# A gate stage's last pair: product and embedding in interleaved halves, the embedding weight's split parts kept in memory, the short tile's embedding packed

## The chip, the cores and the metric

One core of a Trainium2 chip runs the kernel. Its engines work at the same time and wait for each other by semaphores: PE (TensorE, matrix products, with PEld for its weight loads), DVE (VectorE), ACT (ScalarE), POOL (GpSimd) and SP (SyncE, which here only issues DMAs). The metric is device microseconds of one execution, as the median of several runs.

## The reference

One layer over 2048 prompt frames and 32 decode frames, D = 1024, in fp32:

```python
h = h + concat([yA, yB]) @ w_out            # yA, yB: mixers on rmsnorm(h) @ w_in
gate = sigmoid(rmsnorm(h, g_ple) @ w_ple_gate)
h = h + (p_i @ w_ple) * gate                # p_i has 256 columns
y = rmsnorm(h, g_final)
```

The mixers (a short gated convolution and a multi-scale pooling) and their states are not touched by the change. It lies in the last three lines: the embedding product `p_i @ w_ple`, the gate product, and the final norm.

## The kernel before

The rows are cut into 17 tiles: 16 of 128 prompt rows (0 to 15) and one of the 32 decode rows (16, "the short tile"). PE works in fp32r, a shorter format than fp32. So an fp32 operand is split into a high part (an ACT cast, L79) and a low remainder (a DVE subtraction, L82), and a product is made of three: high by high, high by low and low by high, all into one PSUM bank of 512 columns.

The stages follow each other in PE's queue: the input projection in three groups of column blocks ([0, 1], [2, 3], [4]) up to about 538 us, the embedding of the first three tiles, the output projection, the embedding of the rest (about 708 to 745 us), the gate stage.

**Embedding.** `embedding_weights` (L1095, called by `early_embedding` in the third group) loads the 256 rows of w_ple as two tiles of 128x1024 and splits each: `wp[k][0]` is the high part, `wp[k][1]` the low part of half k. `embedding_chunks` does the same for the later products ("wq") and once more for the last pair ("wl"). The split activations of tile i lie in memory as `pp_d[i]`, 128x512: part a, half k, row n. `embed_product` (L103) makes one half of a tile, 512 output columns, in 6 matmuls: 2 halves k times 3 products. `embed` evicts each bank by an ACT copy (L142) and stores the tile to `e_d`. For the short tile the stationary operand has 32 columns instead of 128, and its part of `pp_d` is loaded and stored as 4 pieces of 32 numbers in each of 128 rows.

**Gate stage.** First the decode tile (`plain`, `packed`: a 64-column stationary operand holds high and low side by side, L265, then 32 columns, L268). Then seven pairs of tiles (0, 2, ..., 12) in a loop, then `last_pair` with tiles 14 and 15. Each pair takes `seven` (L205): seven half-size products by a Strassen-Winograd scheme, each of 12 matmuls of 512 columns, in three banks X, Y, Z:

- X = A11·W11, copied by ACT as carry c_00 (L1501); Y = A12·W21, to which `out` adds c_00: output (row tile 0, column half 0);
- X += S2·T2, copied as c_01; Z = S1·T1, copied as c_11; Z += S4·W22, `out` with c_01: output (0, 1);
- X += S3·T3, `out` with c_11: output (1, 1); X += A22·T4, `out` with no carry: output (1, 0).

Hooks (`between`) run at numbered steps between the products. `out` of `gate_ops` adds the carry (DVE, L1509), takes the sigmoid (ACT, L1510), multiplies by the embedding row e (L1512) and adds into h (L1513). `done_g` (L1516) ends a tile: square with a sum (ACT), two small POOL operations, one DVE multiply of 128x1024 (L1520), and a store by POOL (L1521). The h rows of the tiles live in a ring, so SP's load of a later h waits for the store of an earlier tile. `prep_g` makes the next pair's operands inside the present pair: PE transposes through `turned` (L1481), and then splits and differences on DVE and ACT.

In `last_pair` (L1541) the embedding of tile 15 isn't taken from `e_d` but multiplied on the spot: 512 columns between S3's and T4's products, and 512 columns in two banks of 256 behind T4. `finish` (L1567) does the multiply and the add into h, `norm` the square (L1575), the product with g_final (L1581), the POOL sums and root (L1585 to L1591), the scaling by the root (DVE L1595, ACT L1597) and the stores (L1596, L1598).

Tile order on each engine is set by a scheduler of the framework; `tc.keep_in_program_order` pins an instruction to its place in the program.

## Time and profile before

| | us |
|---|---|
| median of 3 runs | 923.92 (922.3 to 926.05) |
| the profiled execution, its own time | 925.15 |
| its span in the trace | 923.4 |
| granted TensorE clock, mean | 0.998 |
| last e_l matmul issued, modelled end | 916.06 |

An engine's row in a timeline gives the start, the duration, the line, the operation with output and inputs, and how many instructions were drawn together; in brackets stands how long the engine had been idle before, and what released it. A list of waits says by engine and line for whom it waited: the sum, how often, the longest. Matmuls overlap in PE's pipeline: one of 512 columns shows 0.39 us, while the next starts 0.23 us later, so a group's cost is the distance to the start of the next group.

### The profile page before, as it was taken

The numbers are of one execution on the slowest core, as the hardware profiler recorded it, in microseconds if no ns is written. First come the engines' busy times: TensorE is split into PE (matmuls) and PEld (weight loads), VectorE is DVE, ScalarE is ACT, GpSimd is POOL, SyncE is SP. The second block draws the span as 40 slices with busy tenths as digits, with TensorE's granted clock in tenths as the row PEclk, the third lists the DMA queues.
The fourth block names the chain that finished last, engine by engine and source line by source line (L and its number), as shares of the span: only waits on it lengthen the run. The fifth ranks groups of instructions, "written<-read, shape, count | busy, mean of one in ns | idle before, by whom it ended". The sixth has DMA issues, their size and how long they took to land.

```text
span 923.4 us, 13197 instructions
## 1 busy us (share of the span) xinstructions
PE 908.2 (98%) x4521; PEld 823.2 (89%) x4521; DVE 723.8 (78%) x1237; ACT 483.5 (52%) x895; POOL 160.5 (17%) x303
## 2 busy tenths in 40 slices
PE   8999999999999999999999999999999999999996
PEld 6999998999999999999999987888878868888885
DVE  6996898999576989795777669665558658889885
ACT  6744565654345555443545446334336755565563
POOL 2111222121000332210000010111203201111123
PEclk9999999999999999999999999999999999999999
DMA  8357687898945799638975359866777964676653
GB/s 245 100 143 218 168 247 224 244 281 283 417 138 170 236 237 229 213 124 292 273 240 171 104 206 270 271 184 186 222 241 232 371 233 137 230 255 199 204 195 114
DMA packets 137679, 201.98 MB, mean 219 GB/s; under 512 B 13116, under 2 KB 101724, under 8 KB 136333
## 3 DMA queue, kind: packets, MB, share of 16 engines
q1 hardware_dynamic: 117581, 138.36, 48.4%
q0 software_dynamic: 17296, 57.35, 19.2%
q10 hardware_dynamic: 2736, 5.44, 1.8%
q8 instruction: 35, 0.57, 0.3%
q14 instruction: 31, 0.25, 0.1%
HBM read 135.55 MB, written 65.54 MB: 218 GB/s over the span
## 4 chain that ended last, share of the span: by engine, by line
PE 76%; DVE 6%; DMA 3%; issue 1%; ACT 1%; POOL 1%; POOLq 0%; DVEq 0%; ACTq 0%
PE x_g L162 9%; PE x_o L162 8%; PE x_zab L574 6%; PE e L106 5%; PE x_zbv L574 5%; PE z_g L162 4%; PE x_ch L574 4%; PE z_o L162 4%; PE z_zab L574 3%; PE z_zbv L574 2%; PE z_ch L574 2%; PE y_g L162 2%; PE y_o L162 2%; PE h L574 2%; PE zb L574 2%; PE c L574 2%
## 5 line engine op out<-in xcount | busy, mean ns | idle before, releaser
L79 ACT CAST y_S<-y_fS 128x512 fp32r<-128x512 f32 x32 | 19.5, 622 | 42.2 <-PE x_o L162 20.4
L162 PE MATMUL x_g<-wg_b,g_S 128*128 128x512 f32 x128 | 36.7, 392 | 0.0
L106 PE MATMUL e<-wq,pps 128*128 128x512 f32 (+1 forms) x156 | 36.2, 391 | 0.1
L162 PE MATMUL x_o<-wo_b,y_S 128*128 128x512 f32 x128 | 35.8, 391 | 0.0
L106 PEld LDWEIGHTS e<-wq,pps 128*128 128x128 f32 (+1 forms) x156 | 28.2, 182 | 7.5 <-issue 0.5
L574 PE MATMUL x_zab<-B,w_zab_S 128*128 128x416 f32 x168 | 34.2, 352 | 0.2 <-ACT V L970 0.2
L574 PE MATMUL z_zab<-B,w_zab_S 128*128 128x416 f32 x168 | 34.3, 351 | 0.0
L574 PE MATMUL x_zbv<-B,w_zbv_S 128*128 128x416 f32 x168 | 34.2, 352 | 0.0
L574 PE MATMUL z_ch<-B,w_ch_S 128*128 128x416 f32 x168 | 34.1, 351 | 0.0
L574 PE MATMUL z_zbv<-B,w_zbv_S 128*128 128x416 f32 x168 | 34.0, 351 | 0.0
L574 PE MATMUL x_ch<-B,w_ch_S 128*128 128x416 f32 x168 | 34.0, 351 | 0.0
L574 PEld LDWEIGHTS x_zab<-B,w_zab_S 128*128 128x128 f32 x168 | 31.3, 188 | 0.9 <-ACT V L970 0.5
L574 PEld LDWEIGHTS x_ch<-B,w_ch_S 128*128 128x128 f32 x168 | 31.4, 188 | 0.3
L574 PEld LDWEIGHTS z_zbv<-B,w_zbv_S 128*128 128x128 f32 x168 | 31.4, 188 | 0.3
L574 PEld LDWEIGHTS z_ch<-B,w_ch_S 128*128 128x128 f32 x168 | 31.3, 188 | 0.3
L574 PEld LDWEIGHTS z_zab<-B,w_zab_S 128*128 128x128 f32 x168 | 31.3, 188 | 0.3
L574 PEld LDWEIGHTS x_zbv<-B,w_zbv_S 128*128 128x128 f32 x168 | 31.3, 188 | 0.4
L79 ACT CAST y<-y 128x512 fp32r<-128x512 f32 x24 | 14.8, 618 | 29.6 <-PE z_o L162 12.8
L71 POOL TENSOR_SCALAR ms_f<-ssq_f 128x1 f32<-128x1 f32 (+1 forms) x15 | 7.6, 509 | 129.4 <-ACT junk L92 129.4
L1315 DVE TENSOR_TENSOR c_o<-x_o,x 128x512 f32<-128x512 f32 x14 | 9.7, 690 | 25.0 <-PE x_o L162 25.0
L162 PEld LDWEIGHTS x_o<-wo_b,y_S 128*128 128x128 f32 x128 | 23.9, 188 | 5.6 <-ACT y_S L79 0.4
L162 PEld LDWEIGHTS x_g<-wg_b,g_S 128*128 128x128 f32 x128 | 23.7, 188 | 4.7
(587 smaller groups left out, 2688.8 us busy)
## 6 DMA issues: line engine op xcount, KB each, us to landing
y<-y_d SPq DMA_DIRECT2D x16, 512.0 KB, 6.0
x<-in_x_prompt_dram SPq DMA_DIRECT2D x16, 512.0 KB, 5.9
h_d<-x SPq DMA_DIRECT2D x16, 512.0 KB, 4.6
h<-h_d SPq DMA_DIRECT2D x16, 512.0 KB, 3.5
xt<-in_x_prompt_dram SPq DMA_DIRECT2D x15, 512.0 KB, 7.1
e<-e_d SPq DMA_DIRECT2D x15, 512.0 KB, 4.8
out_dram<-h POOLq DMA_DIRECT2D x14, 512.0 KB, 3.1
p_dT<-T POOLq DMA_DIRECT2D x12, 512.0 KB, 6.4
```

Source lines behind the costliest of these rows:

```text
L71: nc.gpsimd.tensor_scalar(ms[:n], ssq[:n], scalar1=1.0 / D, scalar2=EPS, op0=ALU.mult, op1=ALU.add)
L79: ins = nc.scalar.copy(hi, src)
L106: nc.tensor.matmul(ps[:n], pps[:, a, k, :n], wp[k][b][:, cs], start=k + q == 0, stop=k == 1 and q == 2)
L162: nc.tensor.matmul(ps[:n], lhs[:, k, a, :n], w[b][:, k], start=start and k + q == 0, stop=k == KH - 1 and q == 2, skip_group_check=True)
L574: nc.tensor.matmul(ps[:, :NB], lhs[:, k, x], b[:, k, y], start=start and k + q == 0, stop=stop and k == KH - 1 and q == 2, skip_group_chec ...
L1315: add = lambda o, a, b: nc.vector.tensor_tensor(o, a, b, op=ALU.add)
```

## The change

- The short tile: its split activations are laid out so that for each half k the 32 high and the 32 low columns lie side by side; load and store move 128 runs of 512 bytes. `short_embed_product` multiplies the 64 columns by the high part of w_ple and the 32 high ones by its low part: 4 matmuls for each 512 output columns. The eviction is an ACT copy of rows 0 to 31 and a DVE add of rows 32 to 63.
- The split parts of w_ple made in the third group are stored to `wl_d` by four stores of 512 KB on POOL's queue. `last_pair` loads them (two on SP at each of the steps 1 and 2) in place of raw rows, casts and subtractions.
- `last_pair`: T4's product and the following embedding product are made in two parts of 256 columns, in turn (`end`), the sigmoid with them. c_11's copy is kept in program order; row 0's first square and weighing come at step 4, the embedding of the upper half at step 5, and `done_g` of tile 13 moves from behind its pair to step 3 of the last pair.

```diff
--- before.py
+++ after.py
@@ -44,6 +44,7 @@
     h_d = tc.dram_tile([T, D], F32, name="h_d")
     e_d = tc.dram_tile([T, D], F32, name="e_d")
     g_d = tc.dram_tile([D, D], F32, name="g_d")
+    wl_d = [[tc.dram_tile([P, D], F32, name=f"wl_d{k}{h}") for h in range(2)] for k in range(2)]
     x4_d = tc.dram_tile([4, P, D], F32, name="x4_d")
     pp_d = tc.dram_tile([NT, P, 2 * PLE], F32, name="pp_d")
@@ -100,10 +101,10 @@
     def rows_of(pr, sa, r, n):
         return pr[r:r + n] if r < SEQ else sa
-    def embed_product(ps, pps, wp, cs, n=P):
+    def embed_product(ps, pps, wp, cs):
         for k in range(2):
             for q, (a, b) in enumerate(((0, 0), (0, 1), (1, 0))):
-                nc.tensor.matmul(ps[:n], pps[:, a, k, :n], wp[k][b][:, cs], start=k + q == 0, stop=k == 1 and q == 2)
+                nc.tensor.matmul(ps, pps[:, a, k], wp[k][b][:, cs], start=k + q == 0, stop=k == 1 and q == 2)
     def load_ple(t, k):
@@ -112,10 +113,17 @@
             nc.sync.dma_start(t[q * 32:q * 32 + 32], w_ple[r:r + 32])
     def load_pps(t, i, queue):
-        n = tiles[i][1]
-        queue.dma_start(t.rearrange("p a k n -> p (a k) n")[:, :, :n].bitcast(F32),
-                        pp_d[i].rearrange("p (a n) -> p a n", a=4)[:, :, :n])
+        n = 4 * tiles[i][1]
+        queue.dma_start(t.rearrange("p a k n -> p (a k n)")[:, :n].bitcast(F32), pp_d[i, :, :n])
         return t
+    def short_embed_product(ps, pps, wp, cs, n):
+        a = pps.rearrange("p a k n -> p (a k n)")[:, :4 * n].rearrange("p (k m) -> p k m", k=2)
+        for k in range(2):
+            for b, m in ((0, 2 * n), (1, n)):
+                nc.tensor.matmul(ps[:m], a[:, k, :m], wp[k][b][:, cs], start=k + b == 0, stop=k + b == 2,
+                                 skip_group_check=True)
     def embed(todo, wp, ring, queue=nc.sync, loads=nc.sync):
@@ -138,7 +146,12 @@
             for nh in range(2):
                 cs = slice(nh * NH, nh * NH + NH)
                 ps = bank(f"e_{i}_{nh}")
-                embed_product(ps, pps, wp, cs, n)
+                if n < P:
+                    short_embed_product(ps, pps, wp, cs, n)
+                    nc.scalar.copy(o[:n, cs], ps[:n])
+                    nc.vector.tensor_tensor(o[:n, cs], ps[n:2 * n], o[:n, cs], op=ALU.add)
+                    continue
+                embed_product(ps, pps, wp, cs)
                 (nc.vector.tensor_copy if last and nh else nc.scalar.copy)(o[:n, cs], ps[:n])
             (nc.gpsimd if last else queue).dma_start(e_d[r:r + n], o[:n])
@@ -202,7 +215,8 @@
         return A, more
-    def seven(name, A, W, carry, out, between={}, late=False, in_parts=False, first_tile=False):
+    def seven(name, A, W, carry, out, between={}, late=False, in_parts=False, first_tile=False, end=None):
@@ -253,6 +267,9 @@
         if not first_tile:
             right()
         step(6)
+        if end is not None:
+            end(X)
+            return
         product(X, A["22"], W["T4"], P, False)
         out(X, None, (1, 0))
@@ -1099,6 +1116,9 @@
                 load_ple(raw, k)
                 t = [wtile(f"{name}{k}_{h}").rearrange("p k h n -> p (k h n)") for h in range(2)]
                 split(t[0], t[1], raw)
+                for h in range(2):
+                    nc.gpsimd.dma_start(wl_d[k][h], t[h].bitcast(F32))
                 wp.append(t)
             return wp
@@ -1223,16 +1243,16 @@
                     for c in range(2 if w == D else 1):
                         i = a + b + c
                         n = tiles[i][1]
-                        o = s[:, c * 2 * PLE:(c + 1) * 2 * PLE].rearrange("p (a k n) -> p a k n", a=2, k=2)[:, :, :, :n]
+                        flat = s[:, c * 2 * PLE:c * 2 * PLE + 4 * n]
                         if n == P:
+                            o = flat.rearrange("p (a k n) -> p a k n", a=2, k=2)
                             src = v[:, (b + c) * PLE:(b + c + 1) * PLE].rearrange("p (g k r) -> p k g r", g=4, k=2)
                             hi, lo = (o[:, h].rearrange("p k (g r) -> p k g r", g=4) for h in range(2))
                         else:
                             src = v.rearrange("p (k r) -> p k r", k=2)
-                            hi, lo = o[:, 0], o[:, 1]
+                            hi, lo = (flat.rearrange("p (k a n) -> p a k n", a=2, k=2)[:, h] for h in range(2))
                         split(hi, lo, src)
-                        nc.gpsimd.dma_start(pp_d[i].rearrange("p (a n) -> p a n", a=4)[:, :, :n],
-                                            o.rearrange("p a k n -> p (a k) n").bitcast(F32))
+                        nc.gpsimd.dma_start(pp_d[i, :, :4 * n], flat.bitcast(F32))
                     yield
         def at_pace(steps, num, den):
@@ -1493,12 +1513,14 @@
             u = t.rearrange("p (g k t) -> p k g t", g=4, k=KC)
             return u[:, :KH], u[:, KH:]
+        carried = []
         def gate_ops(h, e, n, name, i):
             scale = lambda at: rs_h[:n, i + at[0]:i + at[0] + 1]
             def carry(ps, at):
                 t = st.tile([P, NH], F32, tag="t", name=f"c_{name}_{at[0]}{at[1]}")
-                nc.scalar.copy(t[:n], ps[:n])
+                carried.append(nc.scalar.copy(t[:n], ps[:n]))
                 return t
             def out(ps, c, at):
@@ -1514,9 +1536,9 @@
             return carry, out
-        def done_g(i, h):
+        def done_g(i, h, later=False):
             r, n = tiles[i]
-            rf = sumsq(h, n, f"f{i}")
+            rf = sumsq(h, n, f"f{i}", later=later)
             nc.vector.scalar_tensor_tensor(h[:n], h[:n], rf[:n], g_bc[:n], op0=ALU.mult, op1=ALU.mult)
             nc.gpsimd.dma_start(rows_of(y_p, y_s, r, n), h[:n])
@@ -1538,91 +1560,130 @@
             return carry, out
-        def last_pair(i, A):
+        def last_pair(i, A, before):
             pps = load_pps(ss.tile([P, 2, 2, P], F32R, tag="s", name="pps_l"), i + 1, nc.sync)
             e = load_rows(ya, "e", i, e_d)
...
+            wp = []
+            def chunk(k):
+                t = [cmb.tile([P, KH, 2, P], F32R, tag="c", name=f"wl_{k}_{h}").rearrange("p a b c -> p (a b c)")
+                     for h in range(2)]
+                for h in range(2):
+                    nc.sync.dma_start(t[h].bitcast(F32), wl_d[k][h])
+                wp.append(t)
             h = [load_rows(xh, "h", i + b, h_d) for b in range(2)]
             tt = nc.vector.tensor_tensor
             carry, _ = gate_ops(h, [e], P, f"g{i}", i)
             hg = [ring4(ya, f"hg_{b}") for b in range(2)]
             sums = [[], []]
...
+            fixed = lambda ins: tc.keep_in_program_order(ins)
+            def gated(b, cols, t, ee):
+                tt(t, ee, t, op=ALU.mult)
+                fixed(tt(h[b][:, cols], h[b][:, cols], t, op=ALU.add))
+            def square(b, cols):
+                ssq = sm.tile([P, 1], F32, tag="ssq", name=f"ssq_l{b}_{cols.start}")
+                fixed(nc.scalar.activation(junk[:, cols], h[b][:, cols], AF.Square, scale=D ** -0.5, accum_out=ssq))
+                sums[b].append(ssq)
+                if len(sums[b]) == 1:
                     nc.gpsimd.tensor_scalar(ssq, ssq, scalar1=EPS, scalar2=None, op0=ALU.add)
...
+                else:
+                    nc.gpsimd.tensor_tensor(ssq, ssq, sums[b][-2], op=ALU.add)
+            def weigh(b, cols, eng=nc.vector):
+                fixed(eng.tensor_tensor(hg[b][:, cols], h[b][:, cols], g_bc[:, cols], op=ALU.mult))
+            def root(b):
                 rf = sm.tile([P, 1], F32, tag="rstd", name=f"rstd_l{b}")
...
+                nc.gpsimd.tensor_tensor(rf, sums[b][-1], nhalf, op=ALU.pow)
+                return rf
+            def normed(b, rf):
                 r = tiles[i + b][0]
                 o, y = hg[b], y_p[r:r + P]
                 cut = 5 * P
...
+                fixed(nc.vector.tensor_scalar(o[:, :cut], o[:, :cut], scalar1=rf, scalar2=None, op0=ALU.mult))
                 nc.sync.dma_start(y[:, :cut], o[:, :cut])
...
+                fixed(nc.scalar.activation(o[:, cut:], o[:, cut:], AF.Copy, scale=rf))
                 (nc.scalar if b else nc.gpsimd).dma_start(y[:, cut:], o[:, cut:])
+            cols_of = lambda half: slice(half * NH, half * NH + NH)
+            at_last = {}
+            def sigmoid(o, src, b):
+                return nc.scalar.activation(o, src, AF.Sigmoid, scale=rs_h[:, i + b:i + b + 1])
             def out(ps, c, at):
                 b, half = at
...
+                tt(c, ps, c, op=ALU.add)
+                sigmoid(c, c, b)
+                cs = cols_of(half)
+                if b:
+                    at_last["gate"] = c
+                    return
+                gated(0, cs, c, e[:, cs])
+                if half:
+                    of_first(cs, nc.vector)
+                    at_last["root"] = root(0)
+            def of_first(cs, eng):
+                square(0, cs)
+                weigh(0, cs, eng)
+            def held(ps, at):
+                c = carry(ps, at)
+                if at == (1, 1):
+                    fixed(carried[-1])
+                return c
+            def rest():
+                of_first(cols_of(0), nc.gpsimd)
+            def second(cols):
+                ps = bank(f"e_l{cols.start}")[:, :cols.stop - cols.start]
+                embed_product(ps, pps, wp, cols)
+                return ps
+            def upper_half():
+                gated(1, cols_of(1), at_last["gate"], second(cols_of(1)))
+            def end(X):
+                t = st.tile([P, NH], F32, tag="t", name="g_l")
+                m = NH // 2
+                cs = [slice(o, o + m) for o in (0, m)]
+                for c, part in enumerate(cs):
+                    for k in range(KH):
+                        for a, b in FINE:
+                            nc.tensor.matmul(X[:, part], A["22"][:, k, a], W["T4"][b][:, k, part], start=False,
+                                             stop=k == KH - 1 and (a, b) == FINE[-1], skip_group_check=True)
+                    fixed(sigmoid(t[:, part], X[:, part], 1))
+                    ee = second(part)
+                    if c == 0:
+                        normed(0, at_last["root"])
+                        square(1, cols_of(1))
+                    gated(1, part, t[:, part], ee)
+                    if c == 0:
+                        weigh(1, cols_of(1))
+                for part in cs:
+                    square(1, part)
+                weigh(1, cols_of(0))
+                normed(1, root(1))
+            seven(f"g{i}", A, W, held, out, {1: lambda: chunk(0), 2: lambda: chunk(1), 3: before, 4: rest, 5: upper_half}, first_tile=True, end=end)
         def prep_g(i):
@@ -1677,9 +1738,10 @@
             h = [load_rows(xh, "h", i + b, h_d) for b in range(2)]
             e = [load_rows(ya, "e", i + b, e_d) for b in range(2)]
             seven(f"g{i}", A, W, *gate_ops(h, e, P, f"g{i}", i), prep_g(i + 2))
-            for b in range(2):
-                done_g(i + b, h[b])
-        last_pair(NT - 3, S[NT - 3])
+            done_g(i, h[0])
+            if i + 2 < NT - 3:
+                done_g(i + 1, h[1])
+        last_pair(NT - 3, S[NT - 3], lambda: done_g(NT - 4, h[1], True))
```

More of the change, by code (lines that the diff above doesn't have):

```diff
@@ L1553, in last_pair @@
             sums = [[], []]
-            gate = {}
-            def finish(b, half, parts):
-                t = gate[b, half]
-                where = []
-                for cs, ee in parts:
-                    fs = slice(half * NH + cs.start, half * NH + cs.stop)
-                    where.append(fs)
-                    for o, x, op in (t[:, cs], ee, ALU.mult), (h[b][:, fs], h[b][:, fs], ALU.add):
-                        ins = tt(o, x, t[:, cs], op=op)
-                        if len(parts) > 1:
-                            tc.keep_in_program_order(ins)
-                return lambda: norm(b, half, where)
@@ L1572, in norm @@
-            def norm(b, half, where):
-                for fs in where:
-                    ssq = sm.tile([P, 1], F32, tag="ssq", name=f"ssq_l{b}_{fs.start}")
-                    ins = nc.scalar.activation(junk[:, fs], h[b][:, fs], AF.Square, scale=D ** -0.5, accum_out=ssq)
-                    if b:
-                        tc.keep_in_program_order(ins)
-                    sums[b].append(ssq)
-                second = half != b
-                for fs in (where if b == 0 else [*where, slice(half * NH + NH, half * NH + 2 * NH)] if second else []):
-                    ins = (nc.vector if second else nc.gpsimd).tensor_tensor(hg[b][:, fs], h[b][:, fs], g_bc[:, fs], op=ALU.mult)
-                    if b:
-                        tc.keep_in_program_order(ins)
-                if not second:
-                    nc.gpsimd.tensor_scalar(ssq, ssq, scalar1=EPS, scalar2=None, op0=ALU.add)
-                    return
-                if len(where) > 1:
-                    nc.gpsimd.tensor_tensor(sums[b][0], sums[b][0], sums[b][1], op=ALU.add)
-                nc.gpsimd.tensor_tensor(ssq, ssq, sums[b][0], op=ALU.add)
+            fixed = lambda ins: tc.keep_in_program_order(ins)
@@ L1600, in out @@
+            at_last = {}
+            def sigmoid(o, src, b):
+                return nc.scalar.activation(o, src, AF.Sigmoid, scale=rs_h[:, i + b:i + b + 1])
             def out(ps, c, at):
                 b, half = at
-                if c is None:
-                    c, src = st.tile([P, NH], F32, tag="t", name="g_l"), ps
-                else:
-                    tt(c, ps, c, op=ALU.add)
-                    src = c
-                nc.scalar.activation(c, src, AF.Sigmoid, scale=rs_h[:, i + b:i + b + 1])
@@ L1608, in out @@
-                gate[at] = c
-                if b == 0:
-                    finish(b, half, [(slice(0, NH), e[:, half * NH:half * NH + NH])])()
-            def second(half, m):
-                parts = []
-                for o in range(0, NH, m):
-                    ps = bank(f"e_l{half}_{o}")
-                    embed_product(ps[:, :m], pps, wp, slice(half * NH + o, half * NH + o + m))
-                    parts.append((slice(o, o + m), ps[:, :m]))
-                return finish(1, half, parts)
```

8 lines of the change are left out of this document (removed).

## The prediction

> **What bounds the kernel now.** I read the page's shares first, then the waits of PE (TensorE) behind 690 us, where all that changes in PE's queue lies, then the timelines of the last 20 us.
>
> ```profile
> span 923.4 us, 13197 instructions
> PE 908.2 (98%) x4521; PEld 823.2 (89%) x4521; DVE 723.8 (78%) x1237; ACT 483.5 (52%) x895; POOL 160.5 (17%) x303
> ```
>
> ```profile
> PE z_g L162 <- ACT c_g L1501: 0.4, 1, 0.4
> ```
>
> PE is busy for 98%, and from 690 us on it waits once, 0.4 us. So time goes only with PE instructions, with that wait, or in the tail behind the last matmul; work that leaves another engine counts if it reaches one of these. The end:
>
> ```profile
> 901.54 2.88 PE L162 MATMUL z_g<-wg_a,g_S 128*128 128x512 f32 x12
> 904.26 1.07 PE L162 MATMUL x_g<-wg_b,g_S 128*128 128x512 f32 x4
> 905.71 3.03 PE L162 MATMUL z_g<-wg_d,g_S 128*128 128x512 f32 x12 [0.38 <-ACT c_g L1501]
> 908.58 1.98 PE L162 MATMUL x_g<-wg_b,g_S 128*128 128x512 f32 x8
> 910.39 1.52 PE L106 MATMUL e_l<-wl,pps_l 128*128 128x512 f32 x6
> 911.75 2.88 PE L162 MATMUL x_g<-wg_T,g 128*128 128x512 f32 x12
> 914.47 1.59 PE L106 MATMUL e_l<-wl,pps_l 128*128 128x256 f32 x12
> ...
> 904.46 0.63 ACT L1575 ACTIVATE junk<-h 128x512 bf16<-128x512 f32 x1 [1.18 <-DVE h L1567]
> 905.09 0.56 ACT L1501 COPY c_g<-z_g 128x512 f32<-128x512 f32 x1
> 911.59 0.73 ACT L1607 ACTIVATE c_g<-c_g,rs_h 128x512 f32<-128x512 f32 x1 [1.36 <-DVE c_g L1605]
> 912.24 0.63 ACT L1575 ACTIVATE junk<-h 128x512 bf16<-128x512 f32 x1
> 916.37 0.42 ACT L1575 ACTIVATE junk<-h 128x256 bf16<-128x256 f32 x1 [0.40 <-DVE h L1567]
> ...
> 903.60 0.69 DVE L1567 TENSOR_TENSOR h<-h,c_g 128x512 f32<-128x512 f32 x1
> 915.46 0.42 DVE L1567 TENSOR_TENSOR g_l<-e_l,g_l 128x256 f32<-128x256 f32 x1 [0.32 <-ACT g_l L1607]
> 915.91 0.42 DVE L1567 TENSOR_TENSOR h<-h,g_l 128x256 f32<-128x256 f32 x1
> 916.26 0.41 DVE L1567 TENSOR_TENSOR g_l<-e_l,g_l 128x256 f32<-128x256 f32 x1
> 916.71 0.42 DVE L1567 TENSOR_TENSOR h<-h,g_l 128x256 f32<-128x256 f32 x1
> 917.16 0.42 ACT L1575 ACTIVATE junk<-h 128x256 bf16<-128x256 f32 x1 [0.28 <-DVE h L1567]
> 919.16 0.55 DVE L1595 TENSOR_SCALAR hg<-hg,rstd_l 128x640 f32<-128x640 f32 x1 [0.73 <-POOL rstd_l L1591]
> ```
>
> The wait: the S4 product of the last pair needs bank Z, whose copy c_11 (905.09, ACT) stands behind a square (904.46) that waited for DVE's add of 903.60. The z matmuls were fed to 904.42 (901.54 + 2.88), so the copy could have run earlier. The tail: PE ends at 916.06 (914.47 + 1.59), but DVE had both 256-column parts in front of it and finished at 917.13; the last square, the sums on POOL and the scaling follow in a row.
>
> **The short tile.** Its embedding loses 4 matmuls of 12.
>
> ```profile
> L106 PE MATMUL e<-wq,pps x156: 387/389/496, 708.7 to 745.1; 128*128 128x512 f32 x144, 128*32 128x512 f32 x12
> 739.67 5.81 PE L106 MATMUL e<-wq,pps 128*128 128x512 f32 x24
> 745.32 1.08 PE L265 MATMUL x_gl<-wg_c,gl_a 128*64 128x512 f32 x4
> 746.24 1.09 PE L268 MATMUL x_gl<-wg_c,gl_a 128*32 128x512 f32 x4
> ```
>
> A matmul with 32 columns in the stationary operand moves 512 columns as a full one does, 0.235 us from start to start (745.32 − 739.67 over 24); the 64-column form that replaces it takes 0.23 (746.24 − 745.32 over 4). The last ones run at 0.227 (2.72 over 12, 911.75 to 914.47). Four fewer: **−0.91 us** (−0.94 at the slower pace). The eviction gains a DVE add of 32x512 for each half; no PE instruction waits for this tile's embedding before the end of the decode tile, and DVE is 78% busy: 0, and at most two adds of 0.69 if both ends met a full queue. Loads and stores of 128 rows by 512 B instead of 512 pieces by 128 B lie off the path: 0.
>
> **The wait.** c_11 is now kept ahead of the row-0 square, so it needs only the end of S1's product: −0.38, and the copy (0.56) is done 0.3 us before PE asks for it at 905.33 (904.26 + 1.07), all earlier by 0.91. **−0.38 us**; 0 if the square still comes first.
>
> **T4 in two parts.** 12 matmuls of 512 columns become 24 of 256. The e_l row of 12 gives (1.59 − 0.28) / 11 = 0.119 each: 24 × 0.119 = 2.86 against 2.72, **+0.14 us**. Bounds: 0 if they ran at exactly half (0.1135), +2.7 if a short one cost what a long one does, which that row speaks against.
> By the Trainium skill ("TensorE: Matmul & The Clock Gate", LDWEIGHTS (loading the stationary operand)), a weight load lasts its columns over 1.2 in ns, 107 for 128 columns. If the 12 extra loads were exposed the sum would be 1.28 us worse; the row's 0.119 a pair leaves no room for that.
>
> Both parts lie in one bank, and the changed order of PE has a wait of the second part for ACT's sigmoid of the first (as in the wait above, where a matmul waits for ACT's copy of its bank). Part one is modelled to end 1.63 after its start (12 × 0.119 + 0.16 of drain + 0.04 as from 914.63 to the sigmoid). A 256-column sigmoid is about 0.52 (0.73 less the 0.21 by which a square shrinks from 0.63 to 0.42). So it ends at +2.15, and PE, after the six embedding matmuls of part one (0.71), asks at +2.14; with 0.06 to wake up (905.09 + 0.56 to 905.71) I take **+0.06**, from 0 to +0.9 (a sigmoid that queues behind the square, rival two).
> The Trainium skill ("PSUM — Partial Sum Buffer", PSUM bank collisions raise a hardware error) says two engines may not touch one bank at once, other columns included; by that rule the wait can't be dropped, only covered, and the sum stays as it is.
>
> **The tail.** The part-one gate (multiply, add, weigh) now runs while PE does part two, so behind the last matmul stand one multiply and one add instead of a queue of four. PE end by the sum: 916.06 − 0.91 − 0.38 + 0.14 + 0.06 = 914.97; multiply at +0.09, add, square at 915.97 instead of 917.16, the rest as before: 1.19 earlier, so **−0.1** beyond PE. What could spoil it: DVE's row-0 scaling now stands ahead of part one's multiply; with the row-0 chain 1.2 earlier it runs at about 912.75 and the 512-wide weighing ends near 914.7, 0.35 before it is needed.
>
> **The embedding weight kept.** Last pair: two ACT casts and two DVE subtractions (1.06 and 1.22 us each) go, at 904.20 one right behind the add that held the wait above. Four 512 KB loads replace eight smaller. The last of the four lands in the slot of S2, free at 900.6 (901.54 − 0.91); even at 6.0 us (below) it lands at 906.7, and its matmuls start at 909.1. Each, and the h load queued behind it on SP, has over 2 us of slack: 0. In the third group:
>
> ```profile
> 532.30 1.22 DVE L82 TENSOR_TENSOR wp<-raw_wp,wp 128x1024 fp32r<-128x1024 f32 x1
> 534.71 0.50 POOL L1084 DMA_DIRECT2D out_dram<-so  x1 [25.87 <-ACT so L1082]
> 541.04 2.21 SPq L317 DMA_DIRECT2D wo_q<-in_w_out_dram  x4
> 559.44 1.42 PE L157 MATMUL y_o<-wo_c,y 128*128 128x512 f32 x5 [0.53 <-ACT wo_c L1388]
> h_d<-x SPq DMA_DIRECT2D x16, 512.0 KB, 4.6
> ```
>
> POOL stands idle there, so four stores issue as the parts are ready, the last at 533.5, ahead of the `so` stores, whose wait (ACT) ends about then. At 4.6 us, as other 512 KB stores, all are down by 538.2, before the next loads at 541.04: 0. If they drag those loads, PE's wait at 559.44 grows, at most by one store, +4.6.
>
> **Moved around in the loop.** In the changed order, for the first two changes of pair, the transposes of the next pair come later in PE's queue, and DVE's add into the odd row h precedes the subtraction that makes the next pair's A11 residue.
>
> ```profile
> 786.77 2.08 SPq L322 DMA_DIRECT2D h<-h_d  x2
> 789.68 0.69 DVE L1512 TENSOR_TENSOR e<-e,c_g 128x512 f32<-128x512 f32 x1 [0.79 <-ACT c_g L1510]
> 790.29 0.68 DVE L82 TENSOR_TENSOR g<-pth,g 128x512 fp32r<-128x512 f32 x1
> 795.09 0.68 DVE L1513 TENSOR_TENSOR h<-h,e 128x512 f32<-128x512 f32 x1
> 797.03 0.57 ACT L1501 COPY c_g<-x_g 128x512 f32<-128x512 f32 x1
> 798.96 0.39 PE L162 MATMUL x_g<-wg_a,g_S 128*128 128x512 f32 x1
> h<-h_d SPq DMA_DIRECT2D x16, 512.0 KB, 3.5
> e<-e_d SPq DMA_DIRECT2D x15, 512.0 KB, 4.8
> y<-y_d SPq DMA_DIRECT2D x16, 512.0 KB, 6.0
> ```
>
> Before, that add stood at 795.09, 5 us behind the load; now it is due at 789.4 (789.68 − 0.91 + 0.6), and the load, issued at 785.86, lands at 789.36 with 3.5 us. What hangs on it is S4's cast, then the copy of 797.03 (until 797.60), needed by PE at 798.96: 1.36 of slack, less 0.6 for the added step, 0.75. **0 us**, and each microsecond of load beyond 4.3 costs one at each of the two places.
>
> **The sum.** −0.91 − 0.38 + 0.14 + 0.06 − 0.1 = −1.2. The profiled execution took 925.15 (923.4 of span and 1.75 around it), so 923.95 by its own time; it lay 1.23 above the median of the three runs, 923.92 (922.3 to 926.05), so **922.7** as a median. That is 0.13%, inside the 0.5% (4.6 us) that a measurement can tell from no change.
>
> **Rivals.**
> *One, the loop waits for the odd row (the other side).* If the two loads take 6.0 like the y loads, each place costs 6.0 − 4.3 = 1.7, together 3.4: 926.1, slower than before. It decides from 4.9 us on (2 × 0.6 eats the gain). For it: e loads of the same size in the same burst take 4.8. Against: the h loads' own median is 3.5.
> *Two, the wait moves instead of going.* The sigmoid of part one queues behind row 0's square, or the copy behind its old square. If that square stays near 912.24 while PE runs ahead, or the c_11 wait stays, 0.4 to 0.9 is given back: about 923.4. For it: the margin at +2.14 is nil. Against: what feeds the square (z and x products) moves up with PE.
> *Three, the weight's stores cost (the kept copy doesn't save what it should).* One store on the path at 559.44: up to +4.6, 927.3; half of it, 925.0. Against: DMA has 2.8 us free before 541.04.
> *Four, more comes off than I count,* as loop waits too small for the list vanish: no row gives it over 1 us; only a disturbed comparison would bring 4.6.
>
> **How the numbers follow.** Forecast 0.57, rival one 0.17, two 0.14, three 0.08, four 0.04. The forecast's own range is 921.8 to 923.6 (its bounds and a third of the spread of the runs). Low 920.9 takes in a run at the lower end of that spread; high 926.0 reaches to rival one at 6.0 and past the middle of three. Slower by over 0.5% (928.5) needs both places beyond 7 us or three with one: 0.08. Faster by 0.5% (919.3), rival four: 0.04. Within: 0.88.
>
> **What would show it.** Eight matmuls instead of 12 with the 32- and 64-column forms, none of them idle; no wait of z_g for c_g in the last pair; T4 as 24 matmuls in 2.9 us with a wait of at most 0.1 for g_l between its halves; the last square 0.9 to 1.0 behind PE's end instead of 1.1; no wait of x_g for a cast or a copy between 745 and 830 us. Any PE wait near 778 or 798, or before 565, proves me wrong by its length.

## The result, and the profile after

| | before | changed |
|---|---|---|
| median | 923.35 us (16 runs, 922.01 to 926.05) | 921.51 us (16 runs, 920.11 to 924.25) |
| ratio to before, 95% interval | | 0.9979, 0.997 to 0.9989 |
| the profiled execution, its own time | 925.15 | 921.02 |
| its span | 923.4 | 919.2 |

The changed kernel is faster by 0.2%, 1.8 us (1.0 to 2.8 by the interval); forecast were 1.2. The two profiled executions differ by 4.1. Of that, 2.78 lie ahead of the short tile's first matmul, a place that shifts by 1.6 between two traces of the changed kernel itself (below). The page of the changed kernel, its PE timeline at the short tile and at the end, and behind the last dots the short tile of before:

```profile
span 919.2 us, 13202 instructions
PE 905.7 (99%) x4529; PEld 822.7 (90%) x4529; DVE 722.4 (79%) x1236; ACT 481.2 (52%) x894; POOL 159.8 (17%) x307
...
739.76 2.01 PE L125 MATMUL e<-wq,pps 128*64 128x512 f32 x8
741.61 1.07 PE L282 MATMUL x_gl<-wg_c,gl_a 128*64 128x512 f32 x4
...
897.64 2.88 PE L175 MATMUL z_g<-wg_a,g_S 128*128 128x512 f32 x12
900.36 1.07 PE L175 MATMUL x_g<-wg_b,g_S 128*128 128x512 f32 x4
901.27 2.98 PE L175 MATMUL z_g<-wg_d,g_S 128*128 128x512 f32 x12
904.09 1.98 PE L175 MATMUL x_g<-wg_b,g_S 128*128 128x512 f32 x8
905.90 1.53 PE L107 MATMUL e_l<-wl,pps_l 128*128 128x512 f32 x6
907.27 1.59 PE L1671 MATMUL x_g<-wg_T,g 128*128 128x256 f32 x12
908.70 0.88 PE L107 MATMUL e_l<-wl,pps_l 128*128 128x256 f32 x6
909.43 1.69 PE L1671 MATMUL x_g<-wg_T,g 128*128 128x256 f32 x12
910.96 0.88 PE L107 MATMUL e_l<-wl,pps_l 128*128 128x256 f32 x6
...
742.54 2.94 PE L106 MATMUL e<-wq,pps 128*32 128x512 f32 x12
```

From the short tile on no instruction of PE carries a wait in brackets any more, and the list of PE's waits behind 690 us is empty. The parts, each the distance between two starts or ends that stand in these rows, in those of the tail below and in those of before. The span is given to 0.1 us, so what ends with it is good to 0.05:

| part | before | changed | difference |
|---|---|---|---|
| start to the short tile's first matmul | 742.54 | 739.76 | -2.78 |
| short tile | 2.78 | 1.85 | -0.93 |
| decode tile and seven pairs, to the last S1 product | 156.22 | 156.03 | -0.19 |
| S1's start to S4's | 4.17 | 3.63 | -0.54 |
| S4's start to T4's | 6.04 | 6.00 | -0.04 |
| T4 and its embedding, to PE's modelled end | 4.31 | 4.57 | +0.26 |
| PE's end to the last add | 1.07 | 0.99 | -0.08 |
| last add to the last store's issue | 2.67 | 2.20 | -0.47 |
| that issue to the end of the span | 3.60 | 4.17 | +0.57 |

From the short tile on the sum is -1.42, from 180.86 to 179.44. This span, "short tile to end", is used below to compare traces, since what lies ahead of it scatters by more than the change is worth.

The tail of the changed kernel (DVE, ACT, POOL, and the issue of the last store), and in the second block the rows of before that answer the last two of them:

```profile
911.95 0.42 DVE L1589 TENSOR_TENSOR g_l<-e_l,g_l 128x256 f32<-128x256 f32 x1 [0.37 <-PE e_l L107]
912.40 0.43 DVE L1590 TENSOR_TENSOR h<-h,g_l 128x256 f32<-128x256 f32 x1
912.87 0.42 ACT L1594 ACTIVATE junk<-h 128x256 bf16<-128x256 f32 x1 [0.83 <-DVE h L1590]
913.52 0.19 POOL L1599 TENSOR_TENSOR ssq_l<-ssq_l,ssq_l 128x1 f32<-128x1 f32 x1 [1.15 <-ACT junk L1594]
...
915.03 0.38 ACTq L1616 DMA_DIRECT2D out_dram<-hg  x1
```

```profile
917.81 0.66 POOL L1589 TENSOR_TENSOR ssq_l<-ssq_l,ssq_l 128x1 f32<-128x1 f32 x1 [0.60 <-ACT junk L1575]
...
919.80 0.38 ACTq L1598 DMA_DIRECT2D out_dram<-hg  x1
```

One multiply and one add stand behind the last matmul, as forecast. The 0.47 between add and store came from elsewhere: the same POOL add of 128x1 takes 0.19 instead of 0.66. Before, DVE was in three 256-column products at that moment; now it has one product left, which ends as POOL begins. That this is the reason was not tried.

The loop, at the second change of pair (DVE, ACT, PE):

```profile
786.99 0.69 DVE L1535 TENSOR_TENSOR h<-h,e 128x512 f32<-128x512 f32 x1 [0.29 <-DMA h<-h_d]
...
794.19 0.57 ACT L1523 COPY c_g<-x_g 128x512 f32<-128x512 f32 x1
...
795.18 0.39 PE L175 MATMUL x_g<-wg_a,g_S 128*128 128x512 f32 x1
```

Rival one's mechanism is there: DVE waits 0.29 for the odd row. What hangs on it, the copy, ends at 794.76 and PE asks at 795.18. Of the forecast slack of 0.75 there remain 0.42, and PE loses nothing.

### The profile page after: what moved, and what is told of

It is laid out like the page before. It is cut to its first block, busy times and chain, and to the rows that moved or that the text cites. A ratio compares the mean times of both kernels' runs of the same rounds, so it can differ in the third digit from the quotient of the medians.

```text
span 919.2 us, 13202 instructions
## 1 busy us (share of the span) xinstructions
PE 905.7 (99%) x4529; PEld 822.7 (90%) x4529; DVE 722.4 (79%) x1236; ACT 481.2 (52%) x894; POOL 159.8 (17%) x307
## 4 chain that ended last, share of the span: by engine, by line
PE 91%; DVE 3%; DMA 2%; ACT 2%; issue 1%; POOL 0%; SPq 0%; POOLq 0%; DVEq 0%; ACTq 0%
PE x_g L175 9%; PE x_o L175 9%; PE x_zab L591 7%; PE x_zbv L591 6%; PE x_ch L591 5%; PE z_g L175 5%; PE e L107 4%; PE z_o L175 4%; PE z_zab L591 3%; PE h L591 3%; PE z_zbv L591 3%; PE z_ch L591 3%; PE b L591 3%; PE za L591 3%; PE zb L591 2%; PE c L591 2%
## 5 line engine op out<-in xcount | busy, mean ns | idle before, releaser
L107 PE MATMUL e<-wq,pps 128*128 128x512 f32 x144 | 33.1, 390 | 0.0
L107 PEld LDWEIGHTS e<-wq,pps 128*128 128x128 f32 x144 | 27.0, 188 | 5.6
L1542 DVE SCALAR_TENSOR_TENSOR h<-h,rstd_f,g_bc 128x1024 f32<-128x1024 f32 (+1 forms) x15 | 19.3, 1284 | 14.0 <-POOL rstd_f L76 14.0
```

The source lines that it names most:

```text
L107: nc.tensor.matmul(ps, pps[:, a, k], wp[k][b][:, cs], start=k + q == 0, stop=k == 1 and q == 2)
L1542: nc.vector.scalar_tensor_tensor(h[:n], h[:n], rf[:n], g_bc[:n], op0=ALU.mult, op1=ALU.mult)
```

## The experiments

Each kernel stands beside runs of the kernel before on its own chip. All are edits of the changed kernel, but for the first and the ninth, which are edits of the kernel before. "S1 to S4" is 3.63 where PE doesn't wait for c_11.

| kernel | median us | ratio to before, interval | short tile to end | S1 to S4 | issue to end |
|---|---|---|---|---|---|
| packed tile alone | 925.43 | 1.0024, 1.0012 to 1.0037 | 183.45 | 5.86 | 3.58 |
| last pair alone | 923.72 | 1.0005, 0.9996 to 1.0014 | 180.63 | 3.63 | 4.20 |
| weight from raw | 923.05 | 0.9994, 0.9985 to 1.0003 | 179.63 | 3.87 | 3.55 |
| square first | 925.26 | 1.0017, 1.0008 to 1.0026 | 181.68 | 5.78 | 4.15 |
| changed, again | 922.61 | 0.9989, 0.998 to 0.9997 | 179.43 | 3.62 | 4.19 |
| stores on SP | 921.46 | 0.9978, 0.9969 to 0.9987 | 178.91 | 3.63 | 3.58 |
| T4 whole | 922.67 | 0.999, 0.9973 to 1.0006 | 179.90 | 3.63 | 4.15 |
| T4's parts adjacent | 923.15 | 0.9998, 0.9989 to 1.0007 | 180.24 | 3.62 | 4.12 |
| packed, norm moved | 925.85 | 1.0013, 1.0002 to 1.0023 | 182.01 | 3.84 | 3.60 |
| norm not moved | 921.41 | 0.9965, 0.9952 to 0.9978 | 179.46 | 3.62 | 4.11 |
| parts pinned | 923.69 | 0.9994, 0.9984 to 1.0003 | 180.89 | 3.63 | 4.18 |
| 384 and 128 columns | 921.82 | 0.997, 0.9958 to 0.9982 | 179.24 | 3.62 | 3.61 |

**The packed short tile alone.**

```diff
-                embed_product(ps, pps, wp, cs, n)
+                if n < P:
+                    short_embed_product(ps, pps, wp, cs, n)
...
```

> The kernel before with the packed short tile alone. Theory A (the gain is in PE's queue at the places named: short tile 0.95, last pair's wait 0.54 with its restart, loop 0.19, less 0.26 for T4 in parts; what else lay between the two profiled executions, 2.75 us ahead of the short tile, is chance): the 8 matmuls of the short tile take about 1.85 us instead of 2.8, the wait of z_g for c_g stays with 0.3 to 0.5, the loop from the decode tile to the last pair's S1 product takes the 156.0 us of the changed kernel, since its order comes with the packing; the time is 1.0 to 1.2 below before. Theory B (the time ahead of the short tile belongs to the change, to the stores of the weight or the packed loads): with the packing alone the first matmul of the short tile would start 1 us or more earlier than in the kernel before only if the packing is what moves it.

The short tile took its 1.85, as theory A has it, and the loop 156.11 (theory A: 156.0), but the kernel is slower than before, by 2.1 us. Neither theory had that. DVE, ACT and PE in the last pair, then two DVE rows of before, and the windows of PE's granted clock (after the sums of DVE, ACT and POOL comes PEclk):

```profile
901.60 1.29 DVE L1532 SCALAR_TENSOR_TENSOR h<-h,rstd_f,g_bc 128x1024 f32<-128x1024 f32 x1 [0.73 <-POOL rstd_f L75]
903.60 1.28 DVE L1532 SCALAR_TENSOR_TENSOR h<-h,rstd_f,g_bc 128x1024 f32<-128x1024 f32 x1 [0.72 <-POOL rstd_f L75]
904.80 0.68 DVE L1617 TENSOR_TENSOR c_g<-y_g,c_g 128x512 f32<-128x512 f32 x1
...
905.52 0.72 ACT L1619 ACTIVATE c_g<-c_g,rs_h 128x512 f32<-128x512 f32 x1 [3.37 <-DVE c_g L1617]
906.15 0.56 ACT L1513 COPY c_g<-z_g 128x512 f32<-128x512 f32 x1
...
903.63 1.07 PE L174 MATMUL x_g<-wg_b,g_S 128*128 128x512 f32 x4
906.77 4.55 PE L174 MATMUL z_g<-wg_d,g_S 128*128 128x512 f32 x12 [2.07 <-ACT c_g L1513]
911.12 2.10 PE L174 MATMUL x_g<-wg_b,g_S 128*128 128x512 f32 x8
```

```profile
900.32 0.68 DVE L1605 TENSOR_TENSOR c_g<-y_g,c_g 128x512 f32<-128x512 f32 x1
...
902.40 1.28 DVE L1520 SCALAR_TENSOR_TENSOR h<-h,rstd_f,g_bc 128x1024 f32<-128x1024 f32 x1
```

```profile
906.00:908.00 2.00, 1.23 (x5) 1.06 (x6) 1.69 (x3) 1.80 (x4) 0.16 (x1) 0.98 0.82 307
908.00:910.00 2.00, 2.00 (x6) 1.50 (x6) 0.93 (x1) 0.59 (x2) 2.00 (x1) 0.50 0.55 217
910.00:912.00 2.00, 2.00 (x8) 1.58 (x7) 0.65 (x1) 0.00 (x0) 0.30 (x2) 0.67 0.00 0
```

Read from the last row upward through the engines: PE waits 2.07 for the copy c_11; the copy stands on ACT behind the sigmoid of c_00; the sigmoid waits for c_00's add; the add stands on DVE behind both multiplies with the norms of tiles 12 and 13, where before it stood ahead of the second. The packing had touched none of these. But with the packed form, 4 matmuls fewer and two adds more, the scheduler ordered the gate stage anew, and in the last pair this order came out worse. Behind the wait the 12 S4 matmuls last 4.55 instead of 2.98: the granted clock falls to 0.50. The trace is that of the slowest of seven executions; from the short tile on it is 2.6 longer than before, half a microsecond more than the medians show.

**The last pair and the kept weight alone.** The packing's hunks taken out of the changed kernel.

> The changed kernel with the short tile as before (6 matmuls for each half, 32 columns), so the kept weight and the new last pair alone. Theory A: the short tile takes 2.8 us again, the loop the 156.2 us of before, no wait of z_g in the last pair, T4 and its embedding 4.57 us; 0.3 to 0.5 below before in all. Theory B: the stores in the third group move what follows: the embedding of the first tiles, the output projection and the rest up to the short tile would be some 2 us shorter here than in the kernel before, and the time 1.5 or more below.

Theory A's parts came as listed (short tile 2.78, loop 156.25, no wait, T4 and embedding 4.59). From the short tile to the end it gains 0.23; the median shows no change. The expected 0.3 to 0.5 came to less: the end of the program, from the last store's issue, is 0.6 longer (4.20), and POOL's shorter sum gives back only 0.47 of it. So the packing alone costs 2, the last pair alone gives nothing measurable, and both together save 1.8 (1.0 when measured again).

**The weight from its raw rows.**

```diff
-            wp = []
-            def chunk(k):
...
+            wp = embedding_chunks("wl")
```

> The changed kernel without the kept weight: no stores in the third group, and the last pair loads the raw rows and splits them (two casts of 1.06 on ACT, two subtractions of 1.22 on DVE). PE's order is the same. Theory A: the kept weight alone is worth nothing on PE's path as long as c_11's copy is ahead of the square: no wait of z_g for c_g over 0.1, time within 0.5 of the changed kernel. Rival: the casts and the subtractions are what made the copy late; then PE waits 0.3 or more for c_g again and the time is 0.5 to 1 above the changed kernel.

No wait for c_11 is listed, but DVE is late for another bank: T4 waits until c_11's add has read X.

```profile
910.20 1.69 PE L1659 MATMUL x_g<-wg_T,g 128*128 128x256 f32 x12 [0.26 <-DVE c_g L1614]
```

In the last pair the raw rows cost 0.24 up to S4 and some 0.5 around T4; at the end of the program they save 0.6. The trace is 0.2 longer than the changed kernel's. The ratio is 0.5 or 1.4 us above the changed kernel's two, with intervals that overlap, so neither side of the expectation is shown by the time; in the trace the kept weight has a gain and a price of nearly the same size.

**The square first.**

```diff
-                    fixed(carried[-1])
...
-                if half:
-                    of_first(cs, nc.vector)
+                of_first(cs, nc.vector if half else nc.gpsimd)
+                if half:
```

> The changed kernel with row 0's first square back where its add is, and c_11's copy not held, so that the copy stands behind the square on ACT. Theory A: the square can't start before the add of 900.75 (as in the changed kernel's trace), the copy follows about 901.5 and ends about 902.05; PE asks at 901.5 (it does one more S3 matmul first), so it waits 0.5 to 0.6, loses 0.7 with the restart, and the time is 0.7 above the changed kernel. Rival: the add is early enough without the splitting of the weight, and no wait over 0.1 shows.

```profile
902.30 0.63 ACT L1594 ACTIVATE junk<-h 128x512 bf16<-128x512 f32 x1 [2.46 <-DVE h L1590]
903.10 1.06 ACT L93 ACTIVATE junk<-h 128x1024 bf16<-128x1024 f32 x1
904.16 0.57 ACT L1523 COPY c_g<-z_g 128x512 f32<-128x512 f32 x1
...
904.78 3.03 PE L175 MATMUL z_g<-wg_d,g_S 128*128 128x512 f32 x12 [1.77 <-ACT c_g L1523]
```

The wait returns, but of 1.77 instead of 0.5: not one square stands ahead of the copy but two, since that of tile 13, moved to step 3, is pinned behind row 0's. In the order of the changed kernel the place of the copy is worth 2.2 us, four times what the wait of before showed.

**The changed kernel again.**

> The changed kernel as it is, beside the next three on one chip. Its time 921.5 again (1.8 below before); in the trace 179.4 us from the short tile's first matmul to the end of the span, no wait of z_g for c_g, an instruction fetch of 0.01 MB behind the last store and 4.2 us from the last store's issue to the end. Theory A (what lies ahead of the short tile is chance): the start of the short tile's first matmul scatters by 1 us or more against the 739.8 us of the first trace. Theory B (the change brings it forward): it is 739.8 again within 0.3.

Short tile to end is 179.43 against 179.44, part by part the same within 0.04. The short tile begins at 741.37 instead of 739.76, a scatter of 1.6, as theory A has it, and the time is 1.0 below before instead of 1.8. So the 1.4 behind the short tile's start repeats, and the medians scatter around it, presumably by what lies ahead.

**The stores on SP's queue.**

```diff
-                    nc.gpsimd.dma_start(wl_d[k][h], t[h].bitcast(F32))
+                    nc.sync.dma_start(wl_d[k][h], t[h].bitcast(F32))
```

> The changed kernel with the four stores of the weight on SP's queue, so that POOL's program is as long as before. All three kernels with the stores on POOL end 4.15 to 4.20 us after the last store's issue, with an instruction fetch in between; the three without end 3.55 to 3.60 after it, without a fetch. Theory: POOL's longer program makes the fetch and it costs 0.6 at the end; then here 3.6 and no fetch, and the time is 0.6 below the changed kernel. Rival: the end is longer for another reason (SP's or PE's program, the loads back): 4.2 again.

The last store's issue to the end is 3.58 again, and the kernel, at 0.9978 of before, ran 1.15 us below the changed one on the same chip; the intervals overlap, the traces differ by 0.52 from the short tile on. SP's waits at the end, of the changed kernel and of this one:

```profile
SPq L1770 <- DMA out_dram<-hg: 2.2, 2, 1.8
SPq L1770 <- PEq L1770: 1.0, 2, 0.8
```

```profile
SPq L1770 <- DMA out_dram<-hg: 1.9, 2, 1.6
SPq L1770 <- PEq L1770: 0.7, 2, 0.5
```

Two halves of 0.3: SP waits longer for the last stores, and then longer for PE's queue at the very end. A window of the DMA queues over the last microseconds shows an instruction fetch in all eight traces with the stores on POOL, and in none of the six without (the row is the changed kernel's):

```profile
q14 instruction: 1, 0.01, 0.3%
```

It lands behind the end of the span, so it is a sign of POOL's longer program, and not shown to be the wait itself.

**T4 whole.**

```diff
-                for c, part in enumerate(cs):
-                    for k in range(KH):
...
+                product(X, A["22"], W["T4"], P, False)
+                fixed(sigmoid(t, X, 1))
+                for c, part in enumerate(cs):
+                    ee = second(part)
```

> The changed kernel with T4's product whole (12 matmuls of 512 columns), one sigmoid of 512, the embedding of 256 and 256 columns behind it as before. Theory A (the interleaving trades PE time for the tail): T4 with its embedding takes 4.31 instead of 4.58 us, but the last add ends 1.4 to 1.6 behind PE's end instead of 1.0, as DVE gets both parts late; the time is 0.1 to 0.4 above the changed kernel. Rival: the interleaving gives nothing, the time is 0.2 to 0.3 below it, by PE's shorter queue.

```profile
907.56 2.89 PE L175 MATMUL x_g<-wg_T,g 128*128 128x512 f32 x12
910.29 1.59 PE L107 MATMUL e_l<-wl,pps_l 128*128 128x256 f32 x12
...
913.12 0.43 DVE L1590 TENSOR_TENSOR h<-h,g_l 128x256 f32<-128x256 f32 x1
```

T4 and its embedding take 4.32, the last add ends 1.67 behind PE: 0.46 longer from the short tile on. Theory A by the trace; the medians (922.67 and 922.61) don't resolve it. By the trace the interleaving is worth about half a microsecond.

**T4's parts adjacent, then pinned.**

```diff
+                for part in cs:
...
+                            fixed(nc.tensor.matmul(X[:, part], A["22"][:, k, a], W["T4"][b][:, k, part], start=False,
...
+                for c, part in enumerate(cs):
+                    ee = second(part)
```

> The changed kernel with the two parts of T4 one right behind the other, and both parts of the embedding after them: nothing covers the sigmoid that lies between the parts in the bank. Theory A (a matmul into the bank waits until ACT has read it): x_g waits 0.6 to 0.75 for g_l between the parts, and the time is 0.6 to 0.9 above the changed kernel. Rival: the wait costs nothing, as the parts lie in different columns: no wait, and the same time.

This one (without the pins) didn't try what it should: the scheduler put five of the six embedding matmuls between the parts. It shows only that the late embedding costs 0.68 behind PE's end. With the pins:

> As the run with both parts of T4 one behind the other, but with PE's order of these matmuls pinned, since there the scheduler had put five of the embedding's six matmuls of part one between the parts, and so covered the sigmoid again. Theory A: PE waits 0.6 to 0.75 for g_l between the parts; PE's end comes 0.7 later than with the parts interleaved. Rival: no wait.

```profile
909.46 1.60 PE L1673 MATMUL x_g<-wg_T,g 128*128 128x256 f32 x12
911.62 1.69 PE L1673 MATMUL x_g<-wg_T,g 128*128 128x256 f32 x12 [0.56 <-ACT g_l L1624]
```

PE waits for the sigmoid of the other columns, 0.56 listed and 0.73 in all (911.62 against 909.46 + 1.43); T4 and its embedding take 5.29, 0.72 more than interleaved. Theory A: the six embedding matmuls between the parts cover a wait for the shared bank, which is there although the columns differ. No run leaves that wait out.

**The packed tile with only the norm moved.** In the kernel before with the packing, the end of tile 13 goes to step 3; nothing else of the new last pair.

> The packed short tile alone (as in the first of these runs, which was 2.1 slower than before) and, of the new last pair, one thing: the end of tile 13 (its square, its multiply with the norm, its store) moved from behind its pair to step 3 of the last pair. Theory: in the first run ACT's copy c_11 stood behind the sigmoid of c_00, whose add stood on DVE behind both 128x1024 multiplies with the norms of tiles 12 and 13; moved, it stands behind one. Then the add comes about 2 us earlier, PE waits 0.2 to 0.5 for c_11 instead of 2.07, the granted clock stays at 1.00 behind the wait instead of falling to 0.50 for 4 us, and the time is 3 to 4 below that run: 921.9 to 922.5. Rival: the wait comes from the splitting of the embedding weight on DVE and ACT, which stays: the wait keeps 1.5 or more.

The wait for c_11 is gone (3.84 from S1 to S4, clock 1.00), so the first chain is right: its one link undone undoes it. But the time is still above before, by 1.8 in the medians and 1.2 by the ratio, and not at the expected 921.9 to 922.5. DVE's queue is late for the next one in line, T4 (PE, then DVE):

```profile
911.02 3.02 PE L174 MATMUL x_g<-wg_T,g 128*128 128x512 f32 x12 [1.10 <-DVE c_g L1617]
...
906.51 1.23 DVE L82 TENSOR_TENSOR wl<-wlr,wl 128x1024 fp32r<-128x1024 f32 x1 [1.87 <-ACT wl L79]
908.48 1.28 DVE L1532 SCALAR_TENSOR_TENSOR h<-h,rstd_f,g_bc 128x1024 f32<-128x1024 f32 x1 [0.75 <-POOL rstd_f L75]
```

Here the rival has its share: the splitting of the weight holds DVE while it waits for ACT's cast, the moved multiply comes behind it, and c_00's and c_11's adds later still. The last add ends 2.26 behind PE instead of the 1.07 of before.

**The norm not moved.** The changed kernel with the end of tile 13 behind its pair.

> The changed kernel with the end of tile 13 back behind its pair. c_11's copy stays ahead of the square on ACT, and only the sigmoid of c_00 no longer stands in front of c_01 and c_11 on another order. Theory: as DVE does c_00's add ahead of both multiplies here, the sigmoid is not held up, PE doesn't wait for c_11 by more than 0.2, and the time is within 0.4 of the changed kernel (922.6 on the chip of the last runs). Rival: the move is needed in this order as well: a wait of 0.5 or more.

No wait; short tile to end 179.46, the changed kernel's. The move does nothing where the rest of the new last pair is there. The interval of its ratio lies below that of the changed kernel's second measurement and overlaps that of the first. No part of the trace behind the short tile differs, so I take no gain from it.

**Parts of 384 and 128 columns.** On the kernel with the stores on SP.

```diff
-                m = NH // 2
-                cs = [slice(o, o + m) for o in (0, m)]
+                cs = [slice(0, 384), slice(384, NH)]
```

> The kernel with the weight's stores on SP, with the parts of the last product of 384 and 128 columns instead of 256 and 256: the work behind the last matmul (multiply, add, square) is half as wide. If a matmul's pace stays in proportion to its columns (0.227 for 512, 0.119 for 256), 128 columns take 0.06 and the 18 matmuls of the second part 1.1 us; the tail is 0.4 shorter, the time 0.3 to 0.4 lower. Rival, by the weight loads (one of 128 columns for each matmul, 0.107 by the Trainium skill's page TensorE: Matmul & The Clock Gate, LDWEIGHTS): no matmul follows faster than 0.107, the second part takes 1.9 us, PE's end comes 0.8 later and the time is 0.4 higher.

```profile
910.75 1.45 PE L1670 MATMUL x_g<-wg_T,g 128*128 128x128 f32 x12
912.04 0.83 PE L107 MATMUL e_l<-wl,pps_l 128*128 128x128 f32 x6
```

Twelve matmuls of 128 columns take 1.29, 0.1075 each, not 0.06: the rival. T4 and its embedding take 5.27, 0.70 more than with equal parts, and the tail gives back 0.37: 0.33 longer on the trace than with equal parts. The medians, from different chips, don't resolve it.

## Why the prediction was right, and where it was not

**The short tile, -0.91:** -0.93, and the eviction's adds were free.

**The wait, -0.38:** -0.54. The mechanism held for this comparison; the size was short by 0.16. The listed wait counts from the modelled end of the last matmul (0.39 shown), but without it the next one would have started 0.23 behind that matmul's start: 905.71 against 904.26 + 4 × 0.227 = 905.17. By the same reading the copy's margin is not 0.3: in the changed kernel c_11's copy ends at 901.15, and S4 starts at 901.27. What I didn't see is that the wait to be removed was not 0.38 any more: in the order that the packing brings it is 2.07, and costs the clock on top. The new last pair doesn't save half a microsecond, it saves the packing from being a loss.

**T4 in parts, +0.14 and +0.06:** +0.26. The first part runs at 1.43 for 12, as the row of 0.119 has it. The second takes 1.53. It starts 0.06 behind the sigmoid's end (sigmoid 908.90 to 909.37, matmul 909.43), so it seems to pay a restart, though the list shows no wait.

**The tail, -0.1 beyond PE:** -0.08 to the last add. Two terms were missing: -0.47 in POOL's sum and +0.57 at the end of the program. That they nearly cancel is luck.

**The kept weight, 0:** two terms again. It takes work from DVE that would delay T4 and the c_11 copy (the raw rows: 0.7 longer from the short tile on than the kernel with the stores on SP, 179.63 against 178.91), and its stores on POOL cost 0.6 at the very end, a place where the prediction looked for nothing.

**The loop, 0:** -0.19 in both traces of the changed kernel, -0.10 to -0.19 in the others with the packing; not explained. Rival one did not come: the load landed 3.85 behind its issue, inside the slack.

**The sum, -1.2:** -1.42 on the trace, 1.8 and 1.0 in the two pairs of medians. The terms that the prediction named make up -1.29 of it; the loop (-0.19), S4 to T4 (-0.04) and the two that nearly cancel (+0.10) are the rest. The prediction had such a gain down as too small to be told from no change; with 16 executions on each side the interval excludes it. **Rival two** (the wait moves) had its place right and its price wrong: put at 0.4 to 0.9, it is 1.8 (square first), 1.1 at T4 (packed, norm moved) or 2.1 and the clock (packed alone). **Rival three** did not come: none of the traces has a longer wait at the output projection's first products, 0.5 in all of them.

**Open:** the start of the short tile. It came at 739.8 to 741.9 in ten traces with the kept weight and at 742.0 to 743.0 in four without. The means of the two groups differ by 1.4, and 1.1 of that is there at 494 us, before the first of the stores. It lies in waits that change from run to run (the first loads, the transposes at 154 us). Whether it belongs to the change was not tried.

## What to carry to other kernels

An edit that removes matmuls can cost time where a scheduler then orders the rest anew: measure each half of a change alone before its gain is booked, since the two halves here were worth +2.1 and +0.4 (the second not clear of noise), and -1.8 or -1.0 together. Pin the copies that free a PSUM bank: in a queue of their engine they inherit every wait that stands ahead of them, and each wait removed hands the place to the next engine in line. And look at the last four microseconds as at any others: which queue issues four more DMAs decided 0.6 us there.

## What the runs showed of the hardware

- A wait of PE can be followed by half its clock. Behind 2.07 us of listed wait (2.46 from start to start, packed alone) the granted clock fell to 0.50 for 3.4 us, by the windows above (0.98, 0.50, 0.67), and seven matmuls in a row followed each other at 0.427 us instead of 0.227. It fell in the same way, also for 3.4 us, in the run with the pinned parts, behind a wait of 1.81 in the input projection:

```profile
141.57 3.65 PE L593 MATMUL x_zbv<-B_T,w_zbv 128*128 128x416 f32 x12 [1.81 <-DVE V L992]
...
144.00:146.00 2.00, 2.00 (x7) 1.92 (x6) 1.98 (x4) 0.84 (x3) 0.00 (x0) 0.50 0.03 7
```

  These are the two longest waits behind the first 20 us in the 14 traces. Behind the next, 1.77 (square first), 1.65 (packed, norm moved) and 1.64 (before), the clock stayed at 1.00. The Trainium skill ("TensorE: Matmul & The Clock Gate", HAM oscillation — how this bites in real kernels) warns of idle gaps over about 3.4 us; here shorter ones were enough. No run varies the length of a wait alone, so what decides between 1.77 and 1.81 stays open.
- With 128 columns of weights for each, a matmul of 512 columns follows the last by 0.227 us, one of 384 by 0.176, one of 256 by 0.119 and one of 128 by 0.1075 (1.29 / 12): from 256 to 128 columns the pace hardly falls. That the weight load sets the floor was not tried by itself; it would agree with the 107 ns of the Trainium skill ("TensorE: Matmul & The Clock Gate", LDWEIGHTS (loading the stationary operand)).
